# Feed-forward first projection: one matmul of 512 columns against the weights' high half in place of two of 256

## The chip, the cores and the metric

The kernel runs on one core of one Trainium2 chip. The metric is the device time of one execution in microseconds, lower is better. The time before is 1459.29 us, the median of 3 runs (1457.54 to 1460.36).

## What is computed

Two transformer blocks in float32 on 256 positions of width 1024: a macaron block of two layers (each feed-forward, mixer, feed-forward) and a second block with sparse attention, retention and a feed-forward. There are five feed-forwards in all. Each is what the change touches:

```python
def swiglu(x, w_in, w_out):
    a, b = jnp.split(x @ w_in, 2, axis=-1)
    return (jax.nn.silu(a) * b) @ w_out
```

with x of 256 x 1024, a and b of 256 x 2816, and the result of 256 x 1024. In the block's first four feed-forwards x is an RMS-normalised input; the normalisation's factor per position is applied after the product.

## The kernel before

**Split numbers.** Every float32 operand is written as the sum of a high half (rounded to `float32r` by a copy on ScalarE) and a low half (the remainder, a subtraction on VectorE), and a product is three matmuls: high by high, low by high, high by low. `mm3` (L268 to L272) issues them; its three lines carry most of TensorE's work. Weights come in chunks of 128 x 1024 numbers (512 KB). `feed_dma` (L219) loads a chunk into one of 4 `raw` buffers over the SP queue, and `feed_cv` (L231) makes `hi` on ACT (L247) and `lo` on DVE (L248), which this text calls a cast of the chunk. Cast chunks live in the `s4` buffers (28 of them, two a chunk). `nxt` (L252) hands over the next chunks in the order of `weight_plan`, and at each call writes some casts ahead, up to `pos["depth"]` chunks: the program is written in the order in which each engine executes it, so the place of a `nxt` call decides where the casts stand in the queues of ACT and DVE. ACT and DVE take their queues strictly in that order.

**The feed-forward** (`ffn`, L694). The 2816 hidden columns are 11 groups of 256, `j` = 0 to 10. Group 0 is done in another form and isn't touched. Each round `j` = 1 to 10 does:

- `pa`: the 256 columns of a, in two halves `i` of 128 columns, each summed over 8 blocks `kk` of x. Here the weights stand still in the array and x moves, 256 positions wide: three matmuls for each `i` and `kk`, 48 in all, into one PSUM bank (`wproj2`, L537).
- `pb_`: the same for b, 48 matmuls.
- `sg`: `pa` times the normalisation's factor (DVE, L745), then SiLU (ACT, L746).
- the second projection of round `j` - 1 (`fpart`): 24 matmuls of 512 columns on the hidden columns `hp[j - 1]`, into the four banks `f`. Rounds 9 and 10 have none; the last three groups are done after the loop, in `pieces`.
- `u`: `sg` times `pb_` (DVE, L761), split into `hh` (ACT, L533) and `hl` (DVE, L534), which make `hp[j]`.

PSUM has 8 banks: `f` holds four, `pa` and `pb_` one each.

During the first four feed-forwards DVE also sums a product of the second block's modulation weights (`ada_step`, L645 to L652), up to three steps a round.

**x.** `Norm` holds the high half `h` and the low half `l` of x as two buffers of 128 x 8 x 256 (`x8`, four of them). The same four buffers serve the mixers' inputs and outputs.

Of the kernel before, what the change touches and what calls it, by code (L numbers as in the profile page):

```python
# [9 lines left out]
F32 = mybir.dt.float32  # L10
# [6 lines left out]
S = 256  # L17
# [162 lines left out]
class Norm:  # L180


    def __init__(self, xh, xl):
        self.h, self.l = xh, xl
        self.r = None
        self.rb = None

# [2 lines left out]
def block_kernel(ctx: ExitStack, tc: tile.TileContext, a: dict, out: bass.AP, upto: int = 99):  # L190
# [13 lines left out]
    def pp():  # L204
        return [pb(), pb()]

    def x8(shape, dt=F32R, name="x8"):
        return wk.tile(shape, dt, tag="x8", name=name, bufs=4)

    def s4(shape, dt=F32, name="s4"):  # L210
        return wk.tile(shape, dt, tag="s4", name=name, bufs=NS4)
# [1 line left out]
    def s2(shape, dt=F32, name="s2"):  # L213
        return wk.tile(shape, dt, tag="s2", name=name, bufs=NS2)
# [180 lines left out]
    class Lazy:  # L395
# [3 lines left out]

        def __init__(self, g):  # L400
            self.g = g
            self.x = Norm(x8([128, 8, S], name="xh"), x8([128, 8, S], name="xl"))
            self.x.r = [None, None]

        def trans(self, t, halves=(0, 1)):
# [31 lines left out]
    class Shifted:  # L437
# [3 lines left out]

        def __init__(self, g, shift, fill):
            self.g, self.sh, self.fill = g, shift, fill
            self.x = Norm(x8([128, 8, S], name="xh"), x8([128, 8, S], name="xl"))

        def trans(self, t, halves=(0, 1)):
            h_trans(self, t, halves)
# [89 lines left out]
    def wproj2(o, chs, x):  # L537

        for i in range(2):
            cs = slice(i * 128, (i + 1) * 128)  # L540
            for half in range(2):
                for k in range(4):
                    kk = 4 * half + k
                    mm3(o[:, i * S:(i + 1) * S], chs[half][0][:, k, cs], chs[half][1][:, k, cs],
                        x.h[:, kk], x.l[:, kk], kk == 0, kk == 7)

    def wp(name, x):
        p = pb()
        wproj2(p, nxt(name, name), x)
        return p  # L550

    def two(z):
        return z.rearrange("p (c s) -> p c s", c=2)
# [128 lines left out]
    def ffn(nz, each=None):  # L682
        x = nz.x
        hp = {}

        def split_h(u):
            hh, hl = s2([128, 2, S], F32R, name="hh"), s2([128, 2, S], F32R, name="hl")
            split_sb(hh, hl, u)
            return hh, hl

        chs = nxt("fa", "fb", "fa", "fb", ahead=False)
        pt, u0 = [], []
        for t in range(2):
            p = pp()  # L694
            ks = KO if t and not nz.early else range(8)
            for n_, kk in enumerate([*ks, None]):
                for g in range(2):
                    if kk is not None:
                        hi, lo = chs[2 * (kk // 4) + g]
                        pe.matmul(p[g][:, :S], x.h[:, kk, tsl(t)], hi[:, kk % 4], start=n_ == 0, stop=False)  # L700
                        pe.matmul(p[g][:, :S], x.h[:, kk, tsl(t)], lo[:, kk % 4], start=False, stop=False)  # L701
                    if n_:
                        k0 = ks[n_ - 1]
                        pe.matmul(p[g][:, :S], x.l[:, k0, tsl(t)], chs[2 * (k0 // 4) + g][0][:, k0 % 4], start=False,  # L704
                                  stop=kk is None)
                if t == 0 and n_ in TB:
                    nz.trans(1, [TB.index(n_)])
            pt.append(p)
            if t == 0:
                nz.spread(1)  # L710
                nz.evac(1)
                nz.scale(1)
                catch_up(CU[2])
        for t in range(2):
            sg = s2([128, S], name="sg")
            act.activation(sg, pt[t][0][:, :S], AF.Silu, scale=1.0 if x.r is None else x.r[t])
            u = s2([128, S], name="u")
            dve.tensor_tensor(u, sg, pt[t][1][:, :S], op=ALU.mult)
            u0.append(u)
        f = None  # L720

        def fpart(j, i, ch, t, n):
            hh, hl = hp[j]
            cs = slice(n * 512, (n + 1) * 512)
            mm3(f[t][n], hh[:, i, tsl(t)], hl[:, i, tsl(t)], ch[0][:, 0, cs], ch[1][:, 0, cs],
                j == 0 and i == 0, j == NJ - 1 and i == 1)

        for j in range(1, NJ):
            if each and j > 1:
                each()  # L730
            pa = wp("fa", x)
            if j == 1:
                nz.rows()
                pr = pb()
                for i in range(2):
                    for t in range(2):
                        pe.transpose(pr[:, i * S + t * 128:i * S + (t + 1) * 128], u0[t][:, i * 128:(i + 1) * 128],
                                     ident)
                hp[0] = split_h(two(pr))
            chb = nxt("fb", "fb")  # L740
            sg = s2([128, 2, S], name="sg")
            if x.rb is None:
                act.activation(sg, two(pa), AF.Silu)
            else:
                dve.tensor_tensor(sg, two(pa), bc2(x.rb), op=ALU.mult)  # L745
                act.activation(sg, sg, AF.Silu)  # L746
            pb_ = pb()
            wproj2(pb_, chb, x)
            if f is None:
                f = [pp(), pp()]  # L750
            if j < NJ - NH + 1:
                for i in range(2):
                    ch = nxt("fo")
                    for t in range(2):
                        for n in range(2):
                            fpart(j - 1, i, ch, t, n)
                hp.pop(j - 1)
            if each:
                ada_sum()
            u = s2([128, 2, S], name="u")  # L760
            dve.tensor_tensor(u, sg, two(pb_), op=ALU.mult)  # L761
            hp[j] = split_h(u)
        cho = nxt(*["fo"] * (2 * NH))

        def pieces(t):
            def part(j, n):
                for i in range(2):
                    fpart(j, i, cho[2 * (j - NJ + NH) + i], t, n)
            return [(lambda j=j, n=n: part(j, n)) for n in range(2) for j in range(NJ - NH, NJ)]
        return f, pieces  # L770


    def even_mixer(nz):
# [85 lines left out]
                side.append(conv_some)  # L859
        pos["depth"] = DEPTH[1][1]  # L860
        act.preload_act_table_set("natural_log_exp_and_others")
        mh, ml = x8([128, 8, S], name="mh"), x8([128, 8, S], name="ml")
        qT, kT = s4([128, 4, S], name="qT"), s4([128, 4, S], name="kT")
        st = {}

# [123 lines left out]
    def odd_mixer(nz):  # L989
# [95 lines left out]
        def decay(l):  # L1085

            n = 64 >> l
            if l % 2 == 0:
                exs[l // 2] = x8([128, 2, 4, S], F32, name="ex")
            ex = exs[l // 2][:, l % 2]  # L1090
            (e0, e1), (c0, c1) = halves(ex, n), halves(cs, n)
            mid = c0[:, :, n - 1:n].to_broadcast([128, 512 // n, n])
# [63 lines left out]
        for f in steps:  # L1156
            f()
        level(7)
        oh, ol = x8([128, 8, S], name="oh"), x8([128, 8, S], name="ol")
        po = [pp(), pp()]  # L1160

        def pov(t, hd):
# [41 lines left out]
    def second(nz):  # L1204
# [157 lines left out]
        for n in range(2):  # L1362
            pv = pp()
            sproj(lambda t: pv[t], "rg", x.h, x.l)
            for t in range(2):
                sv = sg[t][:, n * 512:(n + 1) * 512]
                act.activation(sv, pv[t], AF.Silu)
                pool.tensor_tensor(sv, sv, gw[:, n * 512:(n + 1) * 512], op=ALU.mult)
        oh, ol = x8([128, 8, S], name="oh"), x8([128, 8, S], name="ol")

        def ret_out(t):
            po = pp()
# [136 lines left out]
        f = [pp(), pp()]  # L1509
        sproj(lambda t: f[t][0], "ap", mh, ml, nk=4)  # L1510
        chs = nxt("ap", "ap")
        xh3, xl3 = x8([128, 8, S], name="wh"), x8([128, 8, S], name="wl")
        for t in range(2):
            for i in range(2):
                smm(f[t][1], t, chs[i], 2 * i, 4, mh, ml)
# [125 lines left out]
```

## Time and profile before

| | |
|---|---|
| median of 3 runs | 1459.29 us |
| the profiled execution | 1458.62 us |
| its span in the trace | 1456.9 us |
| TensorE's mean granted clock | 0.997 of full speed |
| PE busy | 1434.3 us, 98% |
| DVE busy | 983.5 us, 68% |
| ACT busy | 763.6 us, 52% |

The profiled execution lies 0.67 us below the median. PE's rows are matmuls, PEld's the loading of their standing operand, which runs beside them. A matmul's end is modelled, so the pace of matmuls is read from the distance of their starts, not from how long one is shown.

### The profile page before, as it was taken

Reading aid. Unit: us, or ns where it says so; the run is one execution under the profiler, and the core shown is the slowest. Engines: PE = TensorE matmul, PEld = TensorE weight load, DVE = VectorE, ACT = ScalarE, POOL = GpSimd, SP = SyncE. Lnnn points to the kernel's source line nnn. Section 1 sums busy time; section 2 is a strip of 40 time slices with the busy share of each in tenths; the row PEclk is TensorE's granted clock in tenths of the full one; section 3 lists DMA queues with packets and bytes.
Section 4 is the critical chain, followed back from the end, with each engine's and each line's share of the span. In section 5 each row is a group of like instructions: output and inputs, shape, how many; then the busy total and the mean of one; then the engine's idle time right before and its main releaser. Section 6 shows DMA issues by size and latency. Waiting matters only on the chain.

```text
span 1456.9 us, 24390 instructions
## 1 busy us (share of the span) xinstructions
PE 1434.3 (98%) x9623; PEld 1311.0 (90%) x9623; DVE 983.5 (68%) x1348; ACT 763.6 (52%) x1182; POOL 247.1 (17%) x311
## 2 busy tenths in 40 slices
PE   9999999999999999999999999999999999999997
PEld 8999989789999999999888999998988877899997
DVE  6777757977776577675596778755695865475542
ACT  6544357875544464443663655445643665565431
POOL 3001024710110211010242100001132230200001
PEclk9999999999999999999999999999999999999999
DMA  8888554249887478774542588753664654387540
GB/s 273 275 270 258 187 163 148 60 123 304 275 255 227 139 262 260 234 234 134 171 147 66 184 285 266 242 172 111 200 205 132 192 170 136 111 277 234 175 129 29
DMA packets 194948, 281.03 MB, mean 193 GB/s; under 512 B 12381, under 2 KB 148241, under 8 KB 194834
## 3 DMA queue, kind: packets, MB, share of 16 engines
q1 hardware_dynamic: 184386, 248.87, 54.3%
q0 software_dynamic: 10048, 30.03, 6.4%
q8 instruction: 75, 1.23, 0.3%
q10 hardware_dynamic: 400, 0.57, 0.1%
q14 instruction: 39, 0.32, 0.1%
HBM read 277.90 MB, written 1.05 MB: 191 GB/s over the span
## 4 chain that ended last, share of the span: by engine, by line
PE 89%; DVE 4%; ACT 3%; DMA 2%; issue 2%; POOL 0%; SPq 0%; POOLq 0%; DVEq 0%
PE pb L270 27%; PE pb L272 27%; PE pb L271 27%; DVE lo L248 2%; PE pb L701 1%; PE pb L700 1%; PE pb L704 1%; ACT hi L247 1%; PE pb L393 1%; DMA raw<-in_ffn_w_out_dram 1%; ACT pt L823 0%; DVE pb L809 0%; DMA raw<-in_ffn_w_in_dram 0%; DVE ex L1083 0%; DMA raw<-in_w_in_dram 0%
## 5 line engine op out<-in xcount | busy, mean ns | idle before, releaser
L248 DVE TENSOR_TENSOR lo<-raw,hi 128x1024 fp32r<-128x1024 f32 (+1 forms) x461 | 550.7, 1222 | 235.5 <-ACT hi L247 201.1
L247 ACT ACTIVATE hi<-raw 128x1024 fp32r<-128x1024 f32 (+1 forms) x472 | 477.0, 1037 | 215.3 <-PE pb L272 69.7
L270 PE MATMUL pb<-xh,hi 128*128 128x256 f32 x1968 | 558.3, 284 | 0.9 <-DVE u L761 0.9
L271 PE MATMUL pb<-xl,hi 128*128 128x256 f32 x1968 | 556.8, 283 | 0.0
L272 PE MATMUL pb<-xh,lo 128*128 128x256 f32 x1968 | 556.8, 283 | 0.0
L270 PEld LDWEIGHTS pb<-xh,hi 128*128 128x128 f32 x1968 | 376.3, 191 | 4.0 <-issue 1.8
L271 PEld LDWEIGHTS pb<-xl,hi 128*128 128x128 f32 x1968 | 376.4, 191 | 2.0
L272 PEld LDWEIGHTS pb<-xh,lo 128*128 128x128 f32 x1968 | 376.3, 191 | 0.2
L270 PE MATMUL pb<-hi,hh 128*128 128x512 f32 x440 | 172.1, 391 | 0.0
L271 PE MATMUL pb<-lo,hh 128*128 128x512 f32 x440 | 171.8, 390 | 0.0
L272 PE MATMUL pb<-hi,hl 128*128 128x512 f32 x440 | 171.2, 389 | 0.0
L642 POOL DMA_DIRECT2D ada<-in_w_ada_dram x96 | 51.6, 540 | 453.7 <-PE pb L272 276.5
L533 ACT ACTIVATE hh<-u 128x512 fp32r<-128x512 f32 x50 | 31.6, 632 | 136.1 <-DVE u L761 134.2
L272 PEld LDWEIGHTS pb<-hi,hl 128*128 128x128 f32 x440 | 82.6, 188 | 17.6
L270 PEld LDWEIGHTS pb<-hi,hh 128*128 128x128 f32 x440 | 82.8, 188 | 15.8
L271 PEld LDWEIGHTS pb<-lo,hh 128*128 128x128 f32 x440 | 82.8, 188 | 15.4
L270 PE MATMUL pb<-hi,xh 128*128 128x512 f32 x224 | 90.8, 405 | 0.0
L272 PE MATMUL pb<-hi,xl 128*128 128x512 f32 x224 | 87.6, 391 | 0.0
L271 PE MATMUL pb<-lo,xh 128*128 128x512 f32 x224 | 87.4, 390 | 0.0
L746 ACT ACTIVATE sg<-sg 128x512 f32<-128x512 f32 x40 | 25.3, 632 | 103.2 <-DVE sg L745 103.2
L647 DVE SCALAR_TENSOR_TENSOR adacc<-ada,sc,adacc 128x512 f32<-128x512 f32 x84 | 63.0, 750 | 2.0
L761 DVE TENSOR_TENSOR u<-sg,pb 128x512 f32<-128x512 f32 x50 | 34.1, 682 | 40.2 <-PE pb L272 39.5
(324 smaller groups left out, 1665.3 us busy)
## 6 DMA issues: line engine op xcount, KB each, us to landing
raw<-in_ffn_w_in_dram SPq DMA_DIRECT2D x176, 512.0 KB, 5.1
raw<-in_ffn_w_out_dram SPq DMA_DIRECT2D x88, 512.0 KB, 4.6
raw<-in_w_in_dram SPq DMA_DIRECT2D x56, 512.0 KB, 4.4
ada<-in_w_ada_dram POOLq DMA_DIRECT2D x96, 256.0 KB, 4.4
raw<-in_gla_w_in_dram SPq DMA_DIRECT2D x24, 512.0 KB, 4.3
raw<-in_w_ffn_gate_dram SPq DMA_DIRECT2D x22, 512.0 KB, 4.5
raw<-in_w_ffn_up_dram SPq DMA_DIRECT2D x22, 512.0 KB, 4.8
raw<-in_w_ffn_down_dram SPq DMA_DIRECT2D x22, 512.0 KB, 3.4
```

The costliest lines, as they stand in the source:

```text
L247: act.activation(hv, r, AF.Copy)
L248: lo_on.tensor_tensor(lv, r, hv, op=ALU.subtract)
L270: pe.matmul(o, lh, rh, start=start, stop=False)
L271: pe.matmul(o, lh, rl, start=False, stop=False)
L272: pe.matmul(o, ll, rh, start=False, stop=stop)
L393: pe.transpose(nz.p[i][:, k * 128:(k + 1) * 128], h[:, t, c0:c0 + 128], ident)
L533: act.activation(hi, full, AF.Copy)
L642: pool.dma_start(t, w_ada[kt * 128:(kt + 1) * 128, cb * 512:(cb + 1) * 512])
L647: dve.scalar_tensor_tensor(ada["acc"], in0=t, scalar=sc[:, kt:kt + 1], in1=ada["acc"], op0=ALU.mult, op1=ALU.add)
L700: pe.matmul(p[g][:, :S], x.h[:, kk, tsl(t)], hi[:, kk % 4], start=n_ == 0, stop=False)
L746: act.activation(sg, sg, AF.Silu)
L761: dve.tensor_tensor(u, sg, two(pb_), op=ALU.mult)
```

## The change

The high and the low half of x become one buffer, `x16` of 128 x 2 x 8 x 256, two of them in the place of four `x8`. In the rounds 1 to 10 of each feed-forward the weights' high half is loaded once and the two halves of x move through behind each other, 512 columns in one matmul (`x.hl[:, :, kk]`), into a whole bank: high by high in its first half, high by low in its second. The weights' low half then moves the high half of x alone, 256 columns, and is added to the bank's first half. So `i` needs a bank of its own, and `pa` and `pb_` take two banks each. From `kk` = 4 on the low half goes first. The bank's two halves are added when they are read: ACT copies the second to SBUF, DVE adds the first (`added`).

`u` and its split are now written right behind `pb_`, ahead of the two `nxt("fo")` of the round. In round 10 they are done in two pieces, one for each `i`. The groups of other products (mixers, group 0 of the feed-forward, second projection) keep their matmuls; only their buffers have new names.

```diff
-    def x8(shape, dt=F32R, name="x8"):
-        return wk.tile(shape, dt, tag="x8", name=name, bufs=4)
+    def x16(name, dt=F32R):
+
+        return wk.tile([128, 2, 8, S], dt, tag="x16", name=name, bufs=2)
...
+    def wsum2(chs, x):
+
+        ps_ = pp()
+        for i in range(2):
+            cs = slice(i * 128, (i + 1) * 128)
+            for kk in range(8):
+                hi, lo = (z[:, kk % 4, cs] for z in chs[kk // 4])
+                steps = [(ps_[i].rearrange("p (u s) -> p u s", u=2), hi, x.hl[:, :, kk]), (ps_[i][:, :S], lo, x.h[:, kk])]
+                for n_, (o, w, m) in enumerate(steps if kk < 4 else steps[::-1]):
+                    pe.matmul(o, w, m, start=kk == n_ == 0, stop=kk == 7 and n_ == 1)
+        return ps_
+
+    def added(p, name):
+        o = s2([128, 2, S], name=name)
+        for i in range(2):
+            act.activation(o[:, i], p[i][:, S:], AF.Copy)
+            dve.tensor_tensor(o[:, i], o[:, i], p[i][:, :S], op=ALU.add)
+        return o
...
-            pa = wp("fa", x)
+            pa = wsum2(nxt("fa", "fa"), x)
...
-            sg = s2([128, 2, S], name="sg")
-            if x.rb is None:
-                act.activation(sg, two(pa), AF.Silu)
-            else:
-                dve.tensor_tensor(sg, two(pa), bc2(x.rb), op=ALU.mult)
-                act.activation(sg, sg, AF.Silu)
-            pb_ = pb()
-            wproj2(pb_, chb, x)
+            sg = added(pa, "sg")
+            if x.rb is not None:
+                dve.tensor_tensor(sg, sg, bc2(x.rb), op=ALU.mult)
+            act.activation(sg, sg, AF.Silu)
+            pb_ = wsum2(chb, x)
+            if j < NJ - 1:
+                u = added(pb_, "u")
+                dve.tensor_tensor(u, sg, u, op=ALU.mult)
+                hp[j] = split_h(u)
...
-            u = s2([128, 2, S], name="u")
-            dve.tensor_tensor(u, sg, two(pb_), op=ALU.mult)
-            hp[j] = split_h(u)
+        j = NJ - 1
+        u = s2([128, 2, S], name="u")
+        hp[j] = s2([128, 2, S], F32R, name="hh"), s2([128, 2, S], F32R, name="hl")
+        for i in range(2):
+            act.activation(u[:, i], pb_[i][:, S:], AF.Copy)
+            dve.tensor_tensor(u[:, i], u[:, i], pb_[i][:, :S], op=ALU.add)
+            dve.tensor_tensor(u[:, i], sg[:, i], u[:, i], op=ALU.mult)
+            split_sb(hp[j][0][:, i], hp[j][1][:, i], u[:, i])
```

What this moves on DVE, in the second feed-forward from `sg` of round 2 to the casts ahead of `sg` of round 3 (`lo` is a cast, `adacc` the modulation's sum, `pb` any PSUM bank). Before:

```order
L745 TENSOR_TENSOR sg<-pb,rb 128x512
L248 TENSOR_TENSOR lo<-raw,hi 128x1024 x4
L761 TENSOR_TENSOR u<-sg,pb 128x512
L534 TENSOR_TENSOR hl<-u,hh 128x512
L647 SCALAR_TENSOR_TENSOR adacc<-ada,sc,adacc 128x512 x3
L248 TENSOR_TENSOR lo<-raw,hi 128x1024 x4
```

The same place with the change:

```order
L568 TENSOR_TENSOR sg<-sg,pb 128x256 x2
L767 TENSOR_TENSOR sg<-sg,rb 128x512
L568 TENSOR_TENSOR u<-u,pb 128x256 x2
L772 TENSOR_TENSOR u<-sg,u 128x512
L539 TENSOR_TENSOR hl<-u,hh 128x512
L253 TENSOR_TENSOR lo<-raw,hi 128x1024 x4
L671 SCALAR_TENSOR_TENSOR adacc<-ada,sc,adacc 128x512 x3
L253 TENSOR_TENSOR lo<-raw,hi 128x1024 x4
```

The four casts that stood between `sg` and `u` now stand behind the whole chain of `sg` and `u`, and four additions of 128 x 256 are new.

The end of the same feed-forward on ACT, from the casts ahead of round 10 to the squares of the closing norm. Before:

```order
L247 ACTIVATE hi<-raw 128x1024 x4
L746 ACTIVATE sg<-sg 128x512
L533 ACTIVATE hh<-u 128x512
L247 ACTIVATE hi<-raw 128x1024 x2
L343 ACTIVATE sq,ss<-pb,rs_y 128x512 x2
```

The same place with the change:

```order
L252 ACTIVATE hi<-raw 128x1024 x4
L567 ACTIVATE sg<-pb 128x256 x2
L768 ACTIVATE sg<-sg 128x512
L789 ACTIVATE u<-pb 128x256
L538 ACTIVATE hh<-u 128x256
L789 ACTIVATE u<-pb 128x256
L538 ACTIVATE hh<-u 128x256
L252 ACTIVATE hi<-raw 128x1024 x2
L348 ACTIVATE sq,ss<-pb,rs_y 128x512 x2
```

The casts keep their places here; the copies of the banks' second halves are new, and `hh` is made in two pieces.

## Rows read from the trace of the kernel before

**Rows 1.** The page: busy time of each engine, share of the span, instructions.
```profile
PE 1434.3 (98%) x9623; PEld 1311.0 (90%) x9623; DVE 983.5 (68%) x1348; ACT 763.6 (52%) x1182; POOL 247.1 (17%) x311
```
**Rows 2.** The page: the chain that ended last, shares by engine.
```profile
PE 89%; DVE 4%; ACT 3%; DMA 2%; issue 2%; POOL 0%; SPq 0%; POOLq 0%; DVEq 0%
```
**Rows 3.** Stretches: the five feed-forwards' rounds; us, then busy time (instructions), granted clock, DMA share, GB/s.
```profile
15.00:190.00 175.00, 174.15 (x1255) 165.11 (x1254) 126.64 (x144) 88.83 (x113) 20.33 (x40) 1.00 0.79 251
334.00:500.00 166.00, 166.00 (x1163) 156.13 (x1162) 119.67 (x134) 78.65 (x89) 13.37 (x25) 1.00 0.76 244
524.00:690.00 166.00, 166.00 (x1162) 156.09 (x1162) 113.90 (x129) 72.97 (x84) 13.42 (x26) 1.00 0.72 226
836.00:1003.00 167.00, 167.00 (x1174) 157.20 (x1173) 115.94 (x131) 79.29 (x91) 9.12 (x17) 1.00 0.73 231
1280.00:1445.00 165.00, 165.00 (x1157) 155.25 (x1156) 85.50 (x84) 71.55 (x82) 3.08 (x3) 1.00 0.55 172
```
**Rows 4.** Timeline, PE and PEld, second feed-forward: start, us, what; idle before and its releaser.
```profile
384.80 0.28 PE L272 MATMUL pb<-xh,lo 128*128 128x256 f32 x1
...
390.45 0.19 PEld L272 LDWEIGHTS pb<-xh,lo 128*128 128x128 f32 x1
390.56 0.28 PE L272 MATMUL pb<-xh,lo 128*128 128x256 f32 x1
390.57 0.19 PEld L270 LDWEIGHTS pb<-hi,hh 128*128 128x128 f32 x1
390.68 0.40 PE L270 MATMUL pb<-hi,hh 128*128 128x512 f32 x1
...
390.92 0.40 PE L271 MATMUL pb<-lo,hh 128*128 128x512 f32 x1
...
396.15 0.28 PE L270 MATMUL pb<-xh,hi 128*128 128x256 f32 x1
...
396.26 0.28 PE L271 MATMUL pb<-xl,hi 128*128 128x256 f32 x1
```
**Rows 5.** Instructions on tile mh (an even mixer's output): duration ns min/median/max.
```profile
L923 ACT ACTIVATE mh<-pb x4: 364/367/376, 273.5 to 293.9; 128x256 fp32r<-128x256 f32 x4
L924 DVE TENSOR_TENSOR ml<-pb,mh x4: 417/421/425, 274.7 to 294.4; 128x256 fp32r<-128x256 f32 x4
```
**Rows 6.** Groups by line, DVE: busy us, mean ns, idle time before and releasers.
```profile
L534 DVE TENSOR_TENSOR hl<-u,hh 128x512 fp32r<-128x512 f32 x50 | 34.6, 693 | 35.3 <-ACT hh L533 35.3
L761 DVE TENSOR_TENSOR u<-sg,pb 128x512 f32<-128x512 f32 x50 | 34.1, 682 | 40.2 <-PE pb L272 39.5 <-ACT sg L746 0.7
...
L745 DVE TENSOR_TENSOR sg<-pb,rb 128x512 f32<-128x512 f32 x40 | 27.4, 684 | 0.0
```
**Rows 7.** Timeline, ACT, second feed-forward: one of its casts that waits for a buffer.
```profile
451.60 1.06 ACT L247 ACTIVATE hi<-raw 128x1024 fp32r<-128x1024 f32 x1 [2.82 <-PE pb L272]
```
**Rows 8.** Timeline, DVE, second feed-forward, round 1: the casts ahead of `sg`.
```profile
335.82 3.50 DVE L248 TENSOR_TENSOR lo<-raw,hi 128x1024 fp32r<-128x1024 f32 x3 [0.26 <-ACT hi L247]
```
**Rows 9.** Timeline, PE, second feed-forward, round 2: the first matmul with a low half.
```profile
345.44 0.28 PE L272 MATMUL pb<-xh,lo 128*128 128x256 f32 x1
```
**Rows 10.** Waits of PE over the whole run: in total, times, longest.
```profile
PE pb L270 <- DVE u L761: 0.9, 1, 0.9
```
**Rows 11.** Timeline, DVE, second feed-forward, rounds 9 and 10.
```profile
475.85 0.69 DVE L761 TENSOR_TENSOR u<-sg,pb 128x512 f32<-128x512 f32 x1 [3.55 <-PE pb L272]
...
479.82 4.63 DVE L248 TENSOR_TENSOR lo<-raw,hi 128x1024 fp32r<-128x1024 f32 x4
484.36 0.69 DVE L745 TENSOR_TENSOR sg<-pb,rb 128x512 f32<-128x512 f32 x1
487.37 0.69 DVE L761 TENSOR_TENSOR u<-sg,pb 128x512 f32<-128x512 f32 x1 [2.33 <-PE pb L272]
```
**Rows 12.** Groups by line, ACT: busy us, mean ns, idle time before and releasers.
```profile
L533 ACT ACTIVATE hh<-u 128x512 fp32r<-128x512 f32 x50 | 31.6, 632 | 136.1 <-DVE u L761 134.2 <-DMA ada<-in_w_ada_dram 1.9
L746 ACT ACTIVATE sg<-sg 128x512 f32<-128x512 f32 x40 | 25.3, 632 | 103.2 <-DVE sg L745 103.2
```

More of the change, by code (lines that the diff above doesn't have):

```diff
@@ L180, with __init__ @@
 class Norm:
-    def __init__(self, xh, xl):
-        self.h, self.l = xh, xl
+    def __init__(self, x):
+        self.hl, self.h, self.l = x, x[:, 0], x[:, 1]
         self.r = None
@@ L205, in pp, with pair @@
         return [pb(), pb()]
-    def x8(shape, dt=F32R, name="x8"):
-        return wk.tile(shape, dt, tag="x8", name=name, bufs=4)
+    def x16(name, dt=F32R):
+        return wk.tile([128, 2, 8, S], dt, tag="x16", name=name, bufs=2)
+    def pair(name):
+        x = x16(name)
+        return x[:, 0], x[:, 1]
     def s4(shape, dt=F32, name="s4"):
@@ L401, in __init__ @@
             self.g = g
-            self.x = Norm(x8([128, 8, S], name="xh"), x8([128, 8, S], name="xl"))
+            self.x = Norm(x16("x"))
             self.x.r = [None, None]
@@ L443, in __init__ @@
             self.g, self.sh, self.fill = g, shift, fill
-            self.x = Norm(x8([128, 8, S], name="xh"), x8([128, 8, S], name="xl"))
+            self.x = Norm(x16("x"))
         def trans(self, t, halves=(0, 1)):
@@ L861, in even_mixer @@
         act.preload_act_table_set("natural_log_exp_and_others")
[L862 removed]
+        mh, ml = pair("m")
         qT, kT = s4([128, 4, S], name="qT"), s4([128, 4, S], name="kT")
@@ L1088, in decay @@
             if l % 2 == 0:
-                exs[l // 2] = x8([128, 2, 4, S], F32, name="ex")
+                if not l:
+                    exs["all"] = x16("ex", F32).rearrange("p u (l h) s -> p u l h s", l=2)
+                exs[l // 2] = exs["all"][:, l // 2 % 2]
             ex = exs[l // 2][:, l % 2]
@@ L1158, in odd_mixer @@
         level(7)
-        oh, ol = x8([128, 8, S], name="oh"), x8([128, 8, S], name="ol")
+        oh, ol = pair("o")
         po = [pp(), pp()]
@@ L1368, in second @@
                 pool.tensor_tensor(sv, sv, gw[:, n * 512:(n + 1) * 512], op=ALU.mult)
-        oh, ol = x8([128, 8, S], name="oh"), x8([128, 8, S], name="ol")
+        oh, ol = pair("o")
         def ret_out(t):
@@ L1511, in second @@
         chs = nxt("ap", "ap")
-        xh3, xl3 = x8([128, 8, S], name="wh"), x8([128, 8, S], name="wl")
+        xh3, xl3 = pair("w")
         for t in range(2):
```

## The prediction

> **What bounds the kernel now.** I read the page first: PE is busy for 98% of the span [rows 1], and the chain that ended last is 89% PE [rows 2]. That could still be an average over stages with other limits, so I read the five feed-forwards apart, since only they change. In their rounds PE is never idle to speak of: 838.14 of 839.00 us, at the full granted clock [rows 3], which is the 2.4 GHz level. DVE is busy for 120 of 166 us in the second of them, ACT for 79, the DMA engines for up to 79% of the time [rows 3]. So a round takes what its matmuls take, and the question is what a matmul costs, and whether DVE and ACT still keep up when PE gets faster and they get more work.
>
> What a matmul costs is the distance of starts. In the second feed-forward, 48 matmuls of 256 columns lie between the starts at 384.80 and 390.56: 120.0 ns each. Then 24 of 512 columns lie between 390.68 and 396.15: 227.9 ns each [rows 4]. At 2.4 GHz 256 columns are 106.7 ns and 512 are 213.3 ns, so a matmul costs 13.3 or 14.6 ns beside its columns, and this part hardly grows with them. Loads of weights are shown 190 ns long but start every 120 ns, beside the matmuls [rows 4]; they cost nothing of their own that the rows show.
>
> **The change, part by part.** The kernel has 5 feed-forwards, 10 rounds, 2 projections, 2 halves `i` and 8 blocks `kk`: 1600 places where three matmuls of 256 columns become one of 512 and one of 256. The columns stay the same, 768; 1600 matmuls and 1600 weight loads go.
>
> 1. *PE.* Each place falls from 3 x 120.0 = 360.0 ns to 227.9 + 120.0 = 347.9 ns: 12.1 ns, in all **19.4 us**. The two widths have not alternated in this trace, so I bound it. Where the widths change, the first 512 takes 0.24 us (390.68 to 390.92) and the first 256 takes 0.11 us (396.15 to 396.26) [rows 4]: 350 ns a place, 16 us in all. The other end is that a place loses the larger of the two fixed parts whole, 14.6 ns: 23 us. I take 19.4, since it comes from the long runs. A round falls from 17.0 us (96 x 120.0 and 24 x 227.9 ns) to 16.6 us.
>
> The Trainium skill (TensorE: Matmul & The Clock Gate, section Back-to-back issue gap) gives N/2.4 + 2.5 ns for the distance of warm matmuls. By it only 2.5 ns a place would be saved, 4.0 us in all. The rows say 13.3 and 14.6 ns in place of 2.5, and the rows decide.
>
> 2. *ACT, added:* four copies of 128 x 256 out of PSUM a round, 367 ns each by the nearest row [rows 5], 1.5 us a round. ACT has 79 of 166 us in use [rows 3]: hidden behind PE.
>
> 3. *DVE, added:* four additions of 128 x 256 with one side in PSUM, 421 ns each [rows 5], 1.7 us a round. The product of `sg` and that of `u` now read SBUF; they stay at about 0.69 us, as `hl`, all from SBUF, takes 693 ns against 682 and 684 with PSUM [rows 6]. DVE had 119.67 us in 166 [rows 3], 9.8 rounds, so 12.2 us a round; it comes to 13.9. Before `hl` it waits 0.7 us for `hh` (35.3 us over 50 [rows 6]), as before: 14.6 of 16.6 us.
>
> 4. *DVE's order.* `u` stands right behind `sg`, so DVE (and ACT with it) waits for the end of `pb_` while the casts are queued behind. A DVE that came to `sg` on time would be through 1.5 us after `pa`'s end (0.37 copy, 0.42 addition, 0.69 product) and wait 4.1 us of `pb_`'s 5.6 us. 14.6 + 4.1 = 18.7 us is more than a round. So DVE falls behind by 2.1 us a round at most, and each microsecond that it is late takes one off that wait: at 2.1 us late it needs just 16.6 us. It settles there. What that costs is the casts' lead over PE, once. In late rounds the lead is as large as the buffers allow: ACT's cast waits for PE to free one, 2.82 us [rows 7]. It is smallest behind a mixer. The three casts from 335.82 on in the second feed-forward's round 1 [rows 8] are, counted along the plan, the two `fa` chunks and the first `fb` chunk of round 2. The first is done a third of 3.50 us later, at 337.0; PE first uses it at 345.44 [rows 9], 8 us on. 8 us less 2.1 for the delay and some 2.5 for the chain that now goes first still leaves 3. I take **0**; with the lead used up it would be a cast's 1.1 us a round in two early rounds of four feed-forwards, 9 us.
>
> Next, the DMA queue: SP loads a chunk when a cast has freed one of 4 buffers, so a held DVE holds loads too. It is held for 2 to 4 us, and four chunks are under way or waiting. No cost taken; it sits in the same 9 us.
>
> 5. *PSUM.* With `f` all 8 banks are in use. `pa` of round `j` + 1 takes the banks of `pa(j)`, whose additions have 11 us from `pa(j)`'s end (`pb_` 5.6, second projection 5.5), and need some 1.5 plus 2.1 us. `pb_` has as long. In rounds 9 and 10, without second projection, it is 5.6 us, still enough. PE waited once for a bank, 0.9 us, for a `u` that stood behind casts [rows 10]; `u` goes first now, so I take **-0.9 us** (the other end: 0).
>
> 6. *Round 10.* `u` was ready on time, waiting for PE [rows 11], and `hp[10]` is needed 12 matmuls of 0.228 us behind `pb_`, 2.7 us. DVE went from `u(9)` at 475.85 to `sg(10)` at 484.36, 8.5 us [rows 11]. Now a copy and an addition (0.37 and 0.42) come ahead of that, and `sg` takes two additions and a product, 1.5 us: 10.8 of the 11.1 us that two projections take, 0.3 us ahead of `pb_`'s end. SiLU takes 0.63 us, `hh` of the full width 0.63 [rows 12]; the half of it, with a product and an `hl` of half width (0.42 each), makes the first piece ready some 1.5 us behind `pb_`, with 1 us to spare. The second piece is needed six matmuls later. I take a quarter of a cast, 0.3 us, in each of five ends: **+1.5 us**; the other end is a whole cast each, 6 us.
>
> 7. *Buffers.* Two `x16` replace four `x8` of the same size, always used in pairs; 0.
>
> Sum against the profiled execution: 1458.62 - 19.4 - 0.9 + 1.5 = 1439.8 us. Its own time is 0.67 us under the median, so **1440.5 us** stands against 1459.29.
>
> **The rivals.**
>
> - *The lead is thin.* The casts behind a mixer come late because ACT and DVE are held. For: 8 us of lead only [rows 8, 9]. Against: the delay ends by itself. +9 us: 1449.5.
> - *Less than the rows' gap is saved.* Of the 13.3 ns only a small part goes with a matmul, the rest with moving 256 positions of x, which stays. For it there is that no row alternates the widths. Against it, 512 columns of one operand pay 14.6 and not twice 13.3 [rows 4]. If 2.5 ns go: 1458.6 - 4.0 = 1454.6, 1455 for the median. The Trainium skill's figure above would give the same.
> - *The break in the moving operand costs.* x now moves in two pieces of 256, 8 KB apart a partition. If the change from one to the other costs what the change of a matmul costs, 13.3 ns, the places gain -1.2 ns: +1.9 us, 1461, within 0.2% of no change. Nothing in the rows moves in two pieces; the second projection's 512 are one piece.
> - *DVE becomes the bound, slower.* The place is DVE's queue in every round. If an addition costs 0.5 us more than its row, four of them take the round over 16.6 us, and lateness no longer helps: beyond the lead, PE waits. It decides from 14.6 + 2.0 us on. At 18.7 us a round, the wait of 4.1 us in full, three feed-forwards behind mixers lose 10 x 2.1 - 8 = 13 us each: 1458.6 - 19.4 + 39 = 1478, 1479 for the median. Against: the additions have near rows within 10 ns of each other [rows 5].
> - *The change doesn't do what it says:* no; the program holds 1600 matmuls fewer.
>
> **How the numbers follow.** 0.2% (2.9 us) is about what a measurement of this kernel tells from no change. Forecast 0.75 (1435 to 1445 by the bounds above), thin lead 0.12, small saving 0.04: faster 0.91. The break 0.05: same. DVE as the bound 0.04: slower. The range takes in the forecast and most of the thin lead: 1435 (23.4 us saved, the wait gone, nothing lost: 1459.3 - 24.3) to 1452.
>
> **What would show it.** PE: 1600 fewer matmuls; starts 0.23 behind a 512 and 0.12 behind a 256, 11.1 us for two projections against 11.5; PE's idle time in the rounds still under 1 us a feed-forward. DVE: busy share of the second feed-forward up by 17 us, the additions at 0.42 us, and a wait for PE of some 2 us before the additions of `u` in each round. Wrong would be: starts of 0.24 or more behind the 512s (the break), waits of PE for `lo` in rounds 1 to 3 behind a mixer (the lead), or waits of PE for the additions (the banks).

## The result: slower, and the profile after

The changed kernel takes 1475.12 us (median of 4 runs) against 1459.82 us: a ratio of 1.0099, with a 95% interval of 1.0085 to 1.0114. It is slower by 1.0%, where 1440.5 us was forecast. The profiled execution is the shortest of the four, 1468.64 us (span 1466.9); the others are at 1474.4 to 1475.9. What follows accounts for its own 10.0 us over the profiled 1458.62 us of before. The others have no trace, but their mean granted clock is on record: 0.988 to 0.991, where the profiled one has 0.992. Over a span of 1467 us that is an estimated 1.5 to 6 us, so the clock can be most of the difference.

The page, busy time of each engine, and the chain that ended last:

```profile
PE 1430.3 (98%) x8023; PEld 1229.5 (84%) x8023; DVE 1060.4 (72%) x1558; ACT 816.5 (56%) x1387; POOL 247.8 (17%) x311
...
PE 65%; DVE 12%; DMA 11%; ACT 8%; issue 4%; POOL 0%; SPq 0%; DVEq 0%; ACTq 0%; POOLq 0%
```

1600 matmuls are gone, and PE is busy for 4 us less than before [rows 1], not 19. It is still busy for 98% of the span, so the share tells nothing. The chain does: PE's part fell from 89% [rows 2] to 65%, and DVE, DMA and ACT came up. PE now waits for others on the path that sets the end. For whom, the waits of PE over the whole run say (in total, times, longest):

```profile
PE pb L561 <- DVE sg L568: 8.1, 4, 3.6
PE pb L275 <- ACT hh L538: 4.0, 4, 1.9
PE pb L1139 <- DVE last L1113: 2.9, 1, 2.9
...
PE pb L308 <- DVE sg L568: 2.0, 1, 2.0
PE pb L561 <- DVE u L568: 1.6, 1, 1.6
```

L561 is the new matmul, L568 the addition in `added`, L308 the transposes that load columns, which take a bank too. PE waits 11.7 us in all for a bank that an addition has not read yet, where it waited 0.9 us [rows 10], and 4.0 us for `hh` at the ends of feed-forwards. That makes +14.8 us. By feed-forward, the waits for additions are 3.6, 3.5, 0, 3.6 and 1.0 us; the third, which has none, is the one that follows another feed-forward directly.

**The pace.** Timeline of PE, second feed-forward, rounds 3 and 4 (start, us, what; idle before and its releaser):

```profile
369.53 0.50 PE L561 MATMUL pb<-x,hi 128*128 128x512 f32 x1 [0.90 <-DVE sg L568]
...
369.98 0.40 PE L561 MATMUL pb<-x,hi 128*128 128x512 f32 x1
...
375.61 0.39 PE L561 MATMUL pb<-x,hi 128*128 128x512 f32 x1
...
389.05 0.47 PE L561 MATMUL pb<-x,hi 128*128 128x512 f32 x1 [2.56 <-DVE sg L568]
...
392.01 0.63 PE L561 MATMUL pb<-x,hi 128*128 128x512 f32 x1
...
392.65 0.63 PE L561 MATMUL pb<-x,hi 128*128 128x512 f32 x1
```

The matmuls at 369.98 and 375.61 are the same step of two projections, 16 places apart: 5.63 us, 352 ns a place. Forecast were 347.9, before it was 360.0. So a place saves 8.1 ns, and 1600 of them **13.0 us**.

**The clock.** At 389.05 PE starts again after a wait, and from then on the same matmuls are further apart: from 392.01 to 392.65 is one place, 0.64 us in place of 0.35. The stretches (us, then busy time of PE, PEld, DVE, ACT, POOL, granted clock, DMA share, GB/s) show the four places in the middle of the run where that is so:

```profile
58.70:65.50 6.80, 5.13 (x16) 4.26 (x17) 4.85 (x7) 4.89 (x8) 0.00 (x0) 0.50 0.65 223
191.80:195.20 3.40, 3.06 (x7) 2.48 (x8) 2.56 (x3) 2.87 (x5) 0.00 (x0) 0.50 0.01 4
...
389.80:393.20 3.40, 3.40 (x13) 2.92 (x12) 1.70 (x5) 1.93 (x5) 0.23 (x1) 0.50 0.85 289
877.90:881.30 3.40, 3.40 (x13) 2.92 (x12) 1.71 (x4) 1.84 (x5) 0.00 (x0) 0.50 1.02 370
```

The granted clock is 0.50 there, the 1.2 GHz level, each time behind waits of PE; in the rounds of the kernel before it is 1.00 throughout [rows 3]. PE is busy for 15.0 us in them, so up to half of that, 7.5 us, is lost. The kernel before had one such stretch ahead of its rounds (8.6 to 12.0 us, up to 1.7 us lost), which this execution has not. PE's other waits come to 12.5 us for 13.8 before, -1.3 us (the odd mixer's at L1139 is longer, 2.9 for 2.1; two of 1.3 us are gone). Sum: 1458.6 - 13.0 + 14.8 + 7.5 - 1.7 - 1.3 = 1464.9 us; the profiled execution took 1468.6, and 3.7 us stay without a name.

**Why the additions come late.** In the kernel before, `sg` was late already. DVE's timeline in the second feed-forward, rounds 1 to 3:

```profile
339.24 0.68 DVE L745 TENSOR_TENSOR sg<-pb,rb 128x512 f32<-128x512 f32 x1
...
360.41 0.69 DVE L745 TENSOR_TENSOR sg<-pb,rb 128x512 f32<-128x512 f32 x1
...
378.15 0.68 DVE L745 TENSOR_TENSOR sg<-pb,rb 128x512 f32<-128x512 f32 x1
```

`pa(2)` began just ahead of 345.44 [rows 9] and took 5.8 us (48 x 0.120), so it was done at 351.1: `sg(2)` came 9.3 us later. A round of PE is 17.0 us, so `sg(3)`, 17.7 us behind, was 10.0 us late. Nobody waited for it, because six banks were in use and the next `pa` took another one. After the change the same rounds read:

```profile
347.20 0.69 DVE L767 TENSOR_TENSOR sg<-sg,rb 128x512 f32<-128x512 f32 x1
...
369.84 0.69 DVE L767 TENSOR_TENSOR sg<-sg,rb 128x512 f32<-128x512 f32 x1
...
389.27 0.69 DVE L767 TENSOR_TENSOR sg<-sg,rb 128x512 f32<-128x512 f32 x1
```

The additions start 0.78 us ahead of these, in rounds 2 and 3 at 369.06 and 388.49. `pa(3)` wants the bank of `pa(2)` as soon as PE is through with `pb_` and the second projection, and gets it 0.90 us late; `pa(4)` gets it 2.56 us late. `pa(3)` ran from 369.53 to 375.2, so `sg(3)` was 13.3 us late, where the bank allows 11.1. From `sg(1)` to `sg(3)` DVE now takes 42.1 us, where it took 38.9, and the four pairs of additions in between are 3.0 us of it: the added work makes the lateness larger, and the missing bank makes PE wait for it.

And DVE makes lateness up more slowly. One late round of before, then one of after, whole, DVE alone:

```profile
392.60 0.69 DVE L745 TENSOR_TENSOR sg<-pb,rb 128x512 f32<-128x512 f32 x1
394.93 2.36 DVE L248 TENSOR_TENSOR lo<-raw,hi 128x1024 fp32r<-128x1024 f32 x2 [1.65 <-ACT hi L247]
397.45 1.23 DVE L248 TENSOR_TENSOR lo<-raw,hi 128x1024 fp32r<-128x1024 f32 x1 [0.16 <-ACT hi L247]
398.60 0.68 DVE L761 TENSOR_TENSOR u<-sg,pb 128x512 f32<-128x512 f32 x1
399.98 0.69 DVE L534 TENSOR_TENSOR hl<-u,hh 128x512 fp32r<-128x512 f32 x1 [0.70 <-ACT hh L533]
400.58 2.32 DVE L647 SCALAR_TENSOR_TENSOR adacc<-ada,sc,adacc 128x512 f32<-128x512 f32 x3
402.82 3.49 DVE L248 TENSOR_TENSOR lo<-raw,hi 128x1024 fp32r<-128x1024 f32 x3
406.23 0.68 DVE L745 TENSOR_TENSOR sg<-pb,rb 128x512 f32<-128x512 f32 x1
```

```profile
404.19 0.75 DVE L568 TENSOR_TENSOR sg<-sg,pb 128x256 f32<-128x256 f32 x2
404.96 0.69 DVE L767 TENSOR_TENSOR sg<-sg,rb 128x512 f32<-128x512 f32 x1
406.63 0.75 DVE L568 TENSOR_TENSOR u<-u,pb 128x256 f32<-128x256 f32 x2 [0.97 <-ACT u L567]
407.41 0.69 DVE L772 TENSOR_TENSOR u<-sg,u 128x512 f32<-128x512 f32 x1
408.80 0.69 DVE L539 TENSOR_TENSOR hl<-u,hh 128x512 fp32r<-128x512 f32 x1 [0.70 <-ACT hh L538]
409.75 3.50 DVE L253 TENSOR_TENSOR lo<-raw,hi 128x1024 fp32r<-128x1024 f32 x3 [0.26 <-ACT hi L252]
413.16 2.32 DVE L671 SCALAR_TENSOR_TENSOR adacc<-ada,sc,adacc 128x512 f32<-128x512 f32 x3
415.40 2.36 DVE L253 TENSOR_TENSOR lo<-raw,hi 128x1024 fp32r<-128x1024 f32 x2
418.13 1.23 DVE L253 TENSOR_TENSOR lo<-raw,hi 128x1024 fp32r<-128x1024 f32 x1 [0.38 <-ACT hi L252]
419.28 0.75 DVE L568 TENSOR_TENSOR sg<-sg,pb 128x256 f32<-128x256 f32 x2
```

The work is the same six casts, three `adacc` and the products, with two pairs of additions more. Before, the round takes 13.6 us, so DVE gains 3.4 us on PE's 17.0. After, it takes 15.1 us and gains 1.5 on PE's 16.6 (the rounds beside it take 15.7 and 16.2, and gain less). Only 1.5 us of the round are additions; DVE also waits 0.97 us for ACT's copy, which stands behind SiLU.

### The profile page after: what moved, and what is told of

Its sections match the earlier page's. It is cut to its first block, busy times and chain, and to the rows that moved or that the text cites. A ratio compares the mean times of both kernels' runs of the same rounds, so it can differ in the third digit from the quotient of the medians.

```text
span 1466.9 us, 21551 instructions
## 1 busy us (share of the span) xinstructions
PE 1430.3 (98%) x8023; PEld 1229.5 (84%) x8023; DVE 1060.4 (72%) x1558; ACT 816.5 (56%) x1387; POOL 247.8 (17%) x311
## 4 chain that ended last, share of the span: by engine, by line
PE 65%; DVE 12%; DMA 11%; ACT 8%; issue 4%; POOL 0%; SPq 0%; DVEq 0%; ACTq 0%; POOLq 0%
PE pb L561 22%; PE pb L275 12%; PE pb L277 12%; PE pb L276 12%; DMA raw<-in_ffn_w_in_dram 6%; DVE lo L253 6%; ACT hi L252 4%; DMA raw<-in_ffn_w_out_dram 2%; DMA raw<-in_w_ffn_up_dram 1%; DVE sg L568 1%; DVE u L568 1%; DVE sg L767 1%; DVE u L772 1%; PE pb L1157 1%; PE pb L398 1%
## 5 line engine op out<-in xcount | busy, mean ns | idle before, releaser
L252 ACT ACTIVATE hi<-raw 128x1024 fp32r<-128x1024 f32 (+1 forms) x472 | 469.5, 1035 | 233.1 <-DMA raw<-in_ffn_w_in_dram 120.6
L561 PE MATMUL pb<-x,hi 128*128 128x512 f32 x1600 | 560.6, 399 | 9.8 <-DVE sg L568 8.1
L561 PE MATMUL pb<-x,lo 128*128 128x256 f32 x1600 | 418.7, 282 | 0.0
L561 PEld LDWEIGHTS pb<-x,hi 128*128 128x128 f32 x1600 | 292.5, 190 | 67.6 <-DVE sg L568 5.5
L561 PEld LDWEIGHTS pb<-x,lo 128*128 128x128 f32 x1600 | 305.1, 191 | 17.5
L275 PE MATMUL pb<-x,hi 128*128 128x256 f32 (+2 forms) x368 | 105.1, 286 | 0.0
L276 PE MATMUL pb<-x,hi 128*128 128x256 f32 (+2 forms) x368 | 104.0, 283 | 0.0
L277 PE MATMUL pb<-x,lo 128*128 128x256 f32 (+2 forms) x368 | 104.0, 283 | 0.0
L275 PE MATMUL pb<-hi,x 128*128 128x512 f32 x224 | 90.7, 405 | 0.0
L277 PE MATMUL pb<-hi,x 128*128 128x512 f32 x224 | 87.6, 391 | 0.0
L276 PE MATMUL pb<-lo,x 128*128 128x512 f32 x224 | 87.4, 390 | 0.0
L275 PEld LDWEIGHTS pb<-x,hi 128*128 128x128 f32 (+2 forms) x368 | 69.3, 188 | 1.5 <-issue 0.8
L568 DVE TENSOR_TENSOR u<-u,pb 128x256 f32<-128x256 f32 x90 | 34.2, 418 | 50.1 <-ACT u L567 50.1
```

The source lines that it names most:

```text
L252: act.activation(hv, r, AF.Copy)
L275: pe.matmul(o, lh, rh, start=start, stop=False)
L276: pe.matmul(o, lh, rl, start=False, stop=False)
L277: pe.matmul(o, ll, rh, start=False, stop=stop)
L561: pe.matmul(o, w, m, start=kk == n_ == 0, stop=kk == 7 and n_ == 1)
L568: dve.tensor_tensor(o[:, i], o[:, i], p[i][:, :S], op=ALU.add)
```

## The experiments

Theories: **A**, the spare bank: `sg` was late all along, and the banks hid it. **B**, the held queue: `u` ahead of the casts holds them and the loads behind them. **C**, the work: copies and additions make DVE and ACT late. The kernel before was measured again beside the experiments, at 1459.1 to 1459.9 us.

**1. Two banks held in the kernel before.**

```diff
                 f = [pp(), pp()]
+                held = pp()
+                for z in held:
+                    pe.matmul(z[:, :8], ident, ident[:, :8], start=True, stop=True)
+            if j == NJ - 1:
+                for z in held:
+                    pe.matmul(z[:, :8], ident, ident[:, :8], start=True, stop=True)
+                held = None
```

> Three theories for the lost time. A (no spare bank): sg was late in the early rounds all along (9.2 us behind the end of pa in round 2 of the second feed-forward of the kernel before), and spare PSUM banks hid it; with all 8 banks taken, PE waits. B (held queue): u ahead of the casts holds the casts, the raw buffers fill, and loads start late. C (more work): the copies and additions themselves make DVE and ACT late. Here the kernel before has two banks held by 8-column matmuls from round 1 to round 10, nothing else. A: PE waits for DVE sg at the first matmuls of fa in rounds 2 to 4 of the feed-forwards, 4 to 10 us in all, and the time is 1463 to 1472 us. B and C: no such waits, 1459 to 1461 us (20 small matmuls cost 1 to 2 us).

Measured: 1481.58 us, ratio 1.0143 (1.0098 to 1.0187). The waits of PE that are new (L769 is the product `u`):

```profile
PE pb L303 <- DVE u L769: 6.3, 1, 6.3
PE pb L270 <- DVE u L769: 3.4, 2, 2.1
```

Not a copy, not an addition and no other order, and the time goes up by more than the change cost, and by more than A expected. The waits are for `u`, not for `sg` as expected: in the old order `u` stands behind the casts and comes later still. A run with the banks held and `u` ahead of the casts, as in the change, was not made. B and C alone would have left the time as it was.

**2. `u` ahead of the casts, alone.**

```diff
+            if j < NJ - 1:
+                u = s2([128, 2, S], name="u")
+                dve.tensor_tensor(u, sg, two(pb_), op=ALU.mult)
+                hp[j] = split_h(u)
             if f is None:
...
-            u = s2([128, 2, S], name="u")
...
```

> The kernel before, with u and its split moved ahead of the second projection's casts in rounds 1 to 9; no copies, no additions, PSUM as before. B: ACT's casts wait for transfers for 80 us or more in all (37.5 us before, 120.6 us after), PE waits in the early rounds, 1464 to 1472 us. A and C: 1458 to 1461 us, since banks are spare and no work is added.

Measured: 1459.9 us, ratio 1.0001 (0.9985 to 1.0017). ACT's casts did wait longer for transfers of the first projection's weights (37.5 us before):

```profile
ACT hi L247 <- DMA raw<-in_ffn_w_in_dram: 112.9, 66, 5.3
```

It cost nothing, so with banks spare B is not the cause.

**3. `u` back behind the second projection, in the changed kernel.** The four lines that make `u` and split it go back to the end of the round.

> The changed kernel with u, its copies, additions and split back behind the second projection in rounds 1 to 9; all 8 banks in use as after. B: ACT's casts wait for transfers for under 60 us again, and the time is 1446 to 1456 us (the 12.8 us that the pace saves are kept). A: sg stays as late as before the change (9 us), PE waits for its additions in rounds 2 and 3, 1460 to 1470 us. C: the same as A or worse, up to 1475 us, with the waits spread over all rounds.

Measured: 1471.33 us, ratio 1.008 (1.0048 to 1.0111), some 4 us under the change. The largest wait of PE, and ACT's wait for the first projection's weights, are now

```profile
PE pb L561 <- DVE u L568: 11.7, 3, 7.7
...
ACT hi L252 <- DMA raw<-in_ffn_w_in_dram: 22.0, 30, 2.1
```

The casts wait as little for transfers as B expected (120.6 us in the change), and yet some 12 us of loss stay: with all 8 banks in use, too, the held queue is not what most of the loss comes from. The time is 1 us above A's range and within C's, but the waits for additions are five, not one in every round. As in experiment 1, `u` is what comes last. Either order leaves one late reader that holds a bank.

**4. The new form for projection a alone.**

```diff
-            pb_ = wsum2(chb, x)
+            pb_ = pb()
+            wproj2(pb_, chb, x)
...
-                u = added(pb_, "u")
-                dve.tensor_tensor(u, sg, u, op=ALU.mult)
+                u = s2([128, 2, S], name="u")
+                dve.tensor_tensor(u, sg, two(pb_), op=ALU.mult)
...
```

> The new form for projection a alone: half of the copies and additions, half of the saved matmuls (6.4 us by the measured pace of 352 ns a place), one bank less; u ahead of the casts as after. A: the waits for sg's additions mostly go, 1452 to 1458 us. B: the casts are held as after, 1462 to 1470 us. C: half of the loss, 1460 to 1466 us.

Measured: 1458.68 us, ratio 0.9992 (0.9978 to 1.0007). The waits for additions are gone, as A says. The time is 0.7 us above what A expected: 6.5 us of pace are saved and hardly any of it arrives. Work and banks are both halved here, so it does not part A from C by itself; 9 and 10 vary one at a time.

**5. `sg` ahead of the casts that the chunk fb calls for**, from round 2 on, with `u` back as in 3.

```diff
-            chb = nxt("fb", "fb")
+            if j == 1:
+                chb = nxt("fb", "fb")
             sg = added(pa, "sg")
...
             act.activation(sg, sg, AF.Silu)
+            if j > 1:
+                chb = nxt("fb", "fb")
...
```

> The changed kernel with u back behind the second projection, and sg's additions and SiLU ahead of the casts that the chunk fb calls for, from round 2 on; all 8 banks in use. A: what counts is how late sg's additions come, so PE's waits for them shrink, from 11.7 us (for u) and 3 us (for sg) in the run with u back alone to under 6 us together, 1456 to 1466 us. C: the work is the same and stays late, 1469 to 1475 us.

Measured: 1498.54 us, ratio 1.0262 (1.0232 to 1.0291): the worst of all, and both expectations missed. Waits of PE:

```profile
PE pb L561 <- DVE u L568: 21.6, 5, 10.3
PE pb L275 <- ACT hh L538: 11.0, 4, 4.5
```

The additions of `sg(2)` come earlier, 16.2 us behind those of round 1 in the second feed-forward and not 22.6 as in the change. But the long stretch only moves: those of `sg(3)` come 22.6 us behind, and in between stand the casts and, behind them, the additions of `u(2)`, at 385.08, for which PE waits 3.84 us there. Moving one reader forward moves the lateness to the next one.

**6. x contiguous.** The tile of x becomes 8 x 2 x 256 in place of 2 x 8 x 256, and the views are turned.

```diff
-        return wk.tile([128, 2, 8, S], dt, tag="x16", name=name, bufs=2)
+        x = wk.tile([128, 8, 2, S], dt, tag="x16", name=name, bufs=2)
+        return x.rearrange("p k u s -> p u k s")
...
```

> The changed kernel with x laid out so that the high and the low half of one block stand side by side: the 512 moving columns are one piece of 2 KB a partition and not two pieces 8 KB apart. Nothing else. If the step between the pieces costs the 6 ns by which a 512 is slower than forecast (234 against 227.9), its starts are 228 ns apart again and the time falls by 1600 x 6 = 10 us, to 1463 to 1467 us. If the alternation of widths costs it, 234 stays and the time stays at 1473 to 1477 us.

Measured: 1470.08 us, ratio 1.007 (1.0049 to 1.009). PE's timeline, the same step of two projections as above:

```profile
370.09 0.39 PE L562 MATMUL pb<-x,hi 128*128 128x512 f32 x1
...
375.71 0.40 PE L562 MATMUL pb<-x,hi 128*128 128x512 f32 x1
```

16 places in 5.62 us: 351 ns, as before the turn. The break in the moving operand costs nothing that shows. The median is 5 us under the change's 1475.12, between the two expectations, but the intervals of the two ratios overlap and its profiled execution (1472.64) is above the change's (1468.64), so I read nothing into that.

**7. b new in rounds 5 to 9 alone**, so that a bank is spare in the early rounds and round 10 splits as it did.

```diff
+            new = 4 < j < NJ - 1
+            if new:
                 pb_ = wsum2(chb, x)
...
+            else:
+                pb_ = pb()
+                wproj2(pb_, chb, x)
...
```

> Projection a in the new form in all rounds, b in rounds 5 to 9 alone, u ahead of the casts as after: a bank is spare in rounds 1 to 4 and in round 10, 8 are in use between. 15 of 20 projections are new: 1200 places at 8 ns, 9.6 us. A: sg is late in the early rounds alone, so PE's waits for it go, and round 10 splits as before: 1450 to 1456 us. B: casts are held in the early rounds as after, 1460 to 1468 us.

Measured: 1458.0 us, ratio 0.999 (0.9979 to 1.0002). Of 15.7 us of waits for additions and `hh` 1.0 is left, beside one of 2.7 us behind column loads in the first feed-forward. The time is 2 us above A's range: 9.7 us of pace were saved, and some 1.5 arrive.

**8. Experiments 6 and 7 together.**

> The two last together, b new from round 5 to 9 and x contiguous. If the banks (A) and the step between the pieces are both right, 1443 to 1449 us, faster than the kernel before by 0.7 to 1.1%. If only the banks are right, 1450 to 1456 us; if neither, over 1460 us.

Measured: 1458.1 us, ratio 0.9983 (0.997 to 0.9996). Missed again: the pace did not improve, and the saving is lost in part. By the starts in the timeline, the first feed-forward and what follows it (from round 1's transposes to the next feed-forward) took 288.8 us, against 285.7 in the kernel before: it lost 3 us where it should have gained 2. Its chunks are the first that the run loads, and the DMA share of its early rounds (27 to 110 us) was 0.87 in the kernel before, the highest of the early stretches of the five (0.73 to 0.87). That late chunks are the reason is an argument; no run tests it.

**9. Experiment 4 with the eighth bank held**, by two 8-column matmuls in each feed-forward.

```diff
                 f = [pp(), pp()]
+                held = pb()
+                pe.matmul(held[:, :8], ident, ident[:, :8], start=True, stop=True)
+            if j == NJ - 1:
+                pe.matmul(held[:, :8], ident, ident[:, :8], start=True, stop=True)
+                held = None
```

> The kernel with projection a alone in the new form (1458.7 us, 7 banks in use), with the eighth bank held by two 8-column matmuls in each feed-forward. Not an instruction of its rounds is otherwise changed. A (no spare bank): PE's waits for sg's or u's readers come back in rounds 2 to 4, 1464 to 1475 us. C (more work of the copies and additions): nothing changes, 1458 to 1460 us.

Measured: 1466.04 us, ratio 1.0046 (1.0028 to 1.0065), where it was 0.9992 with the bank free. One bank, and no work, is worth 7 us, as A expected. The waits of PE's new matmul in its profile:

```profile
PE pb L561 <- DVE cols L309: 1.9, 1, 1.9
PE pb L561 <- DVE u L774: 1.8, 1, 1.8
...
PE pb L561 <- DVE sg L568: 0.9, 2, 0.6
```

They are smaller than expected, and a wait of 2.1 us for the column loads was there in experiment 4. The clock adds to them: in the stretches at 0.50 PE is busy for 20.5 us here and for 10.2 us in experiment 4's profile, so up to 5.1 us more is lost. Part of that stands behind waits outside the rounds.

**10. Experiment 4 with the full work.** Copies (times zero) and additions are put ahead of b's product; 7 banks.

```diff
                 u = s2([128, 2, S], name="u")
+                for i in range(2):
+                    act.activation(u[:, i], two(pb_)[:, i], AF.Copy, scale=0.0)
+                    dve.tensor_tensor(u[:, i], u[:, i], two(pb_)[:, i], op=ALU.add)
-                dve.tensor_tensor(u, sg, two(pb_), op=ALU.mult)
+                dve.tensor_tensor(u, sg, u, op=ALU.mult)
```

> The kernel with projection a alone in the new form, with the copies (by a factor of zero) and the additions that projection b would need put in ahead of its product in rounds 1 to 9: ACT and DVE do the work of the full change, PE and PSUM stay as in the run with a alone. A: 1457 to 1461 us, as without them. C: half of the loss or more comes back, 1463 to 1470 us.

Measured: 1481.22 us, ratio 1.0136 (1.0116 to 1.0156). That is above the ranges of A and of C: with one bank spare the work costs 22 us more, so the missing bank alone is not the whole cause. Its largest waits of PE:

```profile
PE pb L275 <- ACT hh L538: 9.1, 7, 3.3
PE pb L561 <- DVE sg L568: 5.0, 4, 2.0
```

Two additions of one late round, at its start and at the next one's:

```profile
411.06 0.74 DVE L568 TENSOR_TENSOR sg<-sg,pb 128x256 f32<-128x256 f32 x2
...
426.87 0.74 DVE L568 TENSOR_TENSOR sg<-sg,pb 128x256 f32<-128x256 f32 x2
```

15.8 us; the rounds behind it take up to 16.6 us, against PE's 16.9. DVE makes up almost nothing, so the lateness of rounds 2 and 3 is carried to round 10, where PE waits for `hh` (9.1 us over the run), and meets the bank limit on the way (5.0 us for `sg`). This chain is somewhat longer than the change's own: both halves of b lie in one bank, and ACT's second copy waits for DVE's first addition (21.9 us over 45). So the 22 us are not the price of the change's work alone.

**11. Experiment 8 with the first feed-forward in the old form** (`nth` counts them).

```diff
+        nth.append(1)
...
-            new = 4 < j < NJ - 1
+            new = 4 < j < NJ - 1 and len(nth) > 1
...
-            pa = wsum2(nxt("fa", "fa"), x)
+            pa = wsum2(nxt("fa", "fa"), x) if len(nth) > 1 else wp("fa", x)
...
```

> The kernel with b new from round 5 to 9 and x contiguous, with the first feed-forward wholly in the old form: there the rounds gained nothing (288.8 us from its first transposes to the next feed-forward, 285.6 before), since its chunks come late from DMA whatever PE does. 60 projections of 16 places at 8.6 ns are left, 8.3 us. If the first one lost what the others saved: 1450 to 1455 us. If the saving is lost in all of them, 1457 to 1460 us.

Measured: 1454.18 us, ratio 0.996 (0.9949 to 0.9972): faster than both kernels. The first feed-forward's stretch is back at 284.9 us; the same stretches of the four others (from round 1's transposes to the next feed-forward, or to the end) take 1060.1 us against 1065.3 before, 5.2 of the 8.3 us that the pace saves there.

**12. The work alone, in the kernel before.**

```diff
...
+            for i in range(2):
+                act.activation(ja, sg[:, i, :192], AF.Copy)
+                dve.tensor_tensor(jd, sg[:, i], sg[:, i], op=ALU.add)
             pb_ = pb()
...
             hp[j] = split_h(u)
+            for i in range(2):
+                act.activation(ja, u[:, i, :192], AF.Copy)
+                dve.tensor_tensor(jd, u[:, i], u[:, i], op=ALU.add)
```

> The kernel before, with four copies more on ACT (128x192 out of sg and u into a tile that nobody reads) and four additions more on DVE (128x256, the same) in each round; PSUM, PE and the order as before. Where DVE is late a round of it should take 14.0 + 4 x 0.42 = 15.7 us in place of 14.0, so it makes up 1.3 us of a PE round of 17.0 and not 3.0. If the work alone costs the time (C), the lateness of the early rounds lasts to round 10 and PE waits for hh there, 1464 to 1475 us. If it costs only together with the missing banks (A), 1459 to 1462 us.

Measured: 1462.13 us, ratio 1.0011 (0.9999 to 1.0023). DVE's late rounds in the second feed-forward take 15.0 to 16.3 us, as expected, and with two banks spare that costs 1.6 us, which can hardly be told from nothing: the upper edge of A, with waits of PE for `hh` and `u` of 0.7 us in all.

What the runs say together:

| kernel | most banks in use | DVE work | time, us |
|---|---|---|---|
| before | 6 | old | 1459.8 |
| 12 | 6 | full | 1462.1 |
| 4 | 7 | half | 1458.7 |
| 10 | 7 | full | 1481.2 |
| 9 | 8 | half | 1466.0 |
| 1 | 8 | old | 1481.6 |
| the change | 8 | full | 1475.1 |

Each is nearly free in one place: the work with two spare banks (12), a bank less with half the work (4). Two banks less are not free even without added work (1, where `u` stands behind the casts), nor is the work with one spare bank (10, whose chain is longer). Work sets how fast lateness is made up, banks set how much lateness PE can bear; the change alters both at once, and how its loss divides between them is not shown. Kernels 4, 9, 10 and the change also save pace (6.5 us in the first three, 13.0 in the change), so their loss is larger by that. The clock takes a good part of what 4 and 7 save. In the profiles of 4 and 7, PE is busy at half clock for 10.2 and 13.2 us, in that of the kernel before for 3.4 us. So up to 3.4 and 4.9 us more are lost, where 6.5 and 9.7 us of pace were saved.

## Why the prediction was wrong, point by point

- **Step 5 failed first.** It said that the additions "need some 1.5 plus 2.1 us" of 11 us. The 2.1 us came from step 4's settled state and not from the trace. The trace of before had the row: `sg(2)` at 360.41, 9.3 us behind the end of `pa(2)`, which follows from [rows 9] and the matmuls' pace. Adding only the 2.1 us of step 4 to the 10.0 us of `sg(3)` gives 12.1 us, over the 11.1 that the bank allows. Measured: 13.3 us, and 11.7 us of waits where -0.9 was forecast. Waits for the additions were one of the prediction's own signs of being wrong. Experiments 1 and 9 show that a bank taken away costs time without any added work.
- **Step 4** looked at the wrong lead. It asked whether a cast is ready when PE needs its chunk (that held: no wait of PE in the rounds names a cast), not whether the queue's other work, `sg`, is on time. It began with a DVE that is on time and let it settle 2.1 us late. In the second feed-forward `sg`'s additions are 13.3 us late in round 3 and still some 5 us in rounds 8 to 10 (in round 9, `pa`'s last matmul starts at 479.53 and they start at 484.63). `u` ahead of the casts alone cost nothing while banks were spare (experiment 2).
- **Step 3**: the prices were right (0.42 us an addition, 0.69 us a product out of SBUF). The "14.6 of 16.6 us" left out DVE's other waits for ACT (in the round above 0.97 us for the copy and 0.64 for casts): 15.1 to 16.2 us measured in the late rounds. That is under 16.6, as forecast, but the early rounds live on the difference, which fell from about 3 us to about 1.
- **Step 1** was mis-sized: 13.0 us in place of 19.4, under its lower bound of 16. A 512 and a 256 in turn take 352 ns, not 347.9, and the break between the halves of x is not the reason (experiment 6). The prediction had the nearer rows: where the widths change, 0.24 and 0.11 us, 350 ns a place, which it took as its lower bound only. The formula of the Trainium skill (TensorE: Matmul & The Clock Gate, section Back-to-back issue gap) gave 4.0 us; what was measured lies between it and the forecast.
- **Step 6** was mis-sized: 4.0 us of waits for `hh` against 1.5, because DVE reaches round 10 late: in the second feed-forward `pb_`'s last matmul starts at 496.38, the first addition of `u` at 498.81.
- **Left out**: the clock. PE's waits were priced at their length. The half clock behind them cost up to 7.5 us more in the profiled execution, half as much as the waits.
- **Steps 2 and 7** held; ACT's copies take 0.37 us and no wait of PE names a buffer of x. The wait at L1139 grew by 0.8 us; it is 2.9 us in every run built on the changed kernel and 2.1 in every run built on the one before. Whether the shared `x16` tile is its cause was not tried.
- **The rivals**: the slower one, DVE as the bound, had the right engine and sign and the wrong mechanism. An addition costs 0.42 us, as its row said, and the lateness falls from 13.3 us in round 3 to some 5 in round 10: DVE does not set the pace of the later rounds, though one of them takes 17.4 us.

The Trainium skill (Perfetto Trace Analysis, Matmul Optimizations) advises to use all 8 PSUM banks. In this kernel the runs differ: with all 8 in use in the rounds none is left for a late reader, and the step from 7 to 8 cost 7 us (experiments 4 and 9).

## What to carry to other kernels

Before a change takes the last free buffers, read in the trace how late each of their readers is already, in the worst rounds and not in the settled ones; a wait that is not there may be hidden by the very buffers that the change uses up. Added work on a helper engine is judged by its slack: not whether a round still fits, but how many rounds it now takes to make up the lateness that a stage starts with. And a new wait of PE costs more than its length where the clock falls behind it, so where a stage has no slack (here the first feed-forward) the change is best left out of it.

## What the runs showed of the hardware

- Matmuls of 512 and 256 columns in turn start 352 ns apart in pairs, 4 ns more than the sum of what each takes in a long run of its own kind (227.9 and 120.0). Whether the moving columns lie in one piece or in two makes no difference (351 ns).
- Behind waits of PE of 1.9 to 3.6 us the granted clock stood at 0.50 for 3.4 or 6.8 us (the rows of stretches above). Not every such wait brought it: the one of 2.9 us at L1139 did not in the changed kernel's profile nor in experiment 4's, and in those of experiments 6, 7 and 9 the same wait of 2.9 us has a stretch at 0.50 beside it: one wait of one length had it in one profile and not in another.
